# Decoder block, one core: first root with tokens on partitions, scale columns on ScalarE, fourth shift on VectorE, own tiles for early gate results, gated operands cast first

## The chip, the cores and the metric

The kernel runs on one core of a Trainium2 chip. The time is device time in microseconds (us) of one execution of the whole program. The engines are TensorE (PE: matmuls, and PEld: the loading of their stationary operands), VectorE (DVE), ScalarE (ACT), GpSimd (POOL), and SyncE (SP), which here issues most of the loads. Each engine works through its own instructions strictly in the order in which the program has them. An instruction that must wait for another engine or for a transfer holds up everything behind it on its own engine, also work whose operands are long there.

## The reference

One decoder layer on 1024 tokens of 1024 channels in float32: a token-mixing sub-layer and a SwiGLU sub-layer, each between two root-mean-square norms and modulated by a vector c (shift, scale and gate columns from `silu(c) @ ada_w + ada_b`).

```python
mod = silu(c) @ ada_w + ada_b
sh1, sc1, ga1, sh2, sc2, ga2 = split(mod, 6)
h = rmsnorm(x, pre_mix_g) * (1 + sc1) + sh1
proj = h @ w_in                         # conv, q/k/v and gate columns
u = depthwise_conv(u_val * sigmoid(u_gate))
y_conv = silu(layernorm(u)) @ w_conv_out
y_att = stick_breaking_attention(q, k, v) @ w_att_out
merged = sigmoid(g_conv) * y_conv + sigmoid(g_att) * y_att
x = x + ga1 * rmsnorm(merged @ w_o, post_mix_g)
h = rmsnorm(x, pre_ffn_g) * (1 + sc2) + sh2
gate, up = split(h @ w_ffn_in, 2)
x = x + ga2 * rmsnorm((silu(gate) * up) @ w_ffn_out, post_ffn_g)
```

## The kernel before

Activations lie transposed in SBUF, channels on the 128 partitions and tokens along the row, so the 1024 by 1024 activation is eight tiles `x0` to `x7`. Products in higher precision are split: an operand is cast on ACT to fp32r (the "hi" half, line 145 for most) and DVE takes the rest (the "lo" half, "operand minus hi"); a product then is three matmuls, hi by hi, hi by lo and lo by hi.

The program is written in an order and then placed by a static scheduler, which decides the order on each engine. Priorities (`tc.high_priority`, `pin`) and scheduling-only dependencies (`add_manual_dep` with `NoSync`, which fix an order and cost no wait on the chip) steer it. Tiles come from pools; a tag with `bufs=2` is a ring of two buffers, and a new tile of that tag waits until the oldest one's last reader is done. Pools are opened and closed one after the other, and what is closed gives its memory to the pools that follow.

Three places matter here.

**The start.** ACT squares x, PE sums the squares over the partitions by matmuls with a matrix of ones (`sums`, line 251, into `pvar`), so the sum of each token stands on all 128 partitions, in two halves of 512 tokens. ACT takes the root from each half, 128 by 512 elements (lines 334 and 335), DVE corrects it by a Newton step of three instructions on 128 by 512 elements for each half (lines 343 to 345) and multiplies x by scale column and root (`x_op`, line 300). ACT adds the shift column and casts (`hi_op`, line 303, tiles `hhi`), and DVE makes the lo half (`lo_op`, line 306, tiles `hlo`). The shift column of each of the eight tiles comes either from PE (`shift_pe`, line 284, with `shift_act` on ACT, line 288) or from a dot product on DVE (`dot_c`, line 121; `SH_DVE` says for which tiles: 5, 6 and 7). The scale columns always come from dot products on DVE, with a small instruction on line 295 behind each.

**The gates.** Gate products use a seven-product scheme for 2 by 2 blocks. `early(i, q)` makes the first of the products for the gate pair i ahead of the rest: a load of the weights (`ew`), a cast on ACT and its lo on DVE (tiles `a`, lines 145 and 414), 12 matmuls into a PSUM tile `k` (line 427), and an ACT instruction that takes the result out of PSUM into a tile `ee` (line 672) and stores it (line 673). There are 14 such results. The `ee` tiles come from the tag `sg`, two buffers that the sigmoid results (line 653) use too. Behind this, in a new pool `pg`, the kernel loads x back (16 loads `f<-xm_d` on SP), combines its parts on DVE (tiles `f`, lines 722 to 725), makes the operands `T1o` to `T4o` of them (cast on ACT, lo on DVE, line 708), and then does the other five products for each gate pair (`other_five`): weights `gw0a`, `gw0b` and so on are loaded, summed on DVE (tiles `gs`, lines 750 to 755), split into the operands `s1o` to `s4o` and `a` (line 414 for the lo), and multiplied with the T tiles on PE into `ka` and `kc`. The layer norm of the convolution branch (`ln_all`) is woven in: loads `cr<-u_d` on SP, sums on DVE (`la`, lines 795 and 797), a matmul `lnm` on PE (line 799), its copy `lm` on ACT (line 800), subtractions on DVE (`cr<-cr,lm`, line 803), squares, a matmul `lnv` (line 809), a root, and products (line 813).

**The FFN's down projection.** It opens with `prep1(j)` for j = 0 to 10: two gated operands `gb` from `X_j` (cast on ACT, lo on DVE, line 1577) and two weight operands `wa` (cast on ACT, lo on DVE, line 1583), then 24 matmuls on line 1591. `X` and `Y` are loaded back from `g_d`, the raw weights `wa` come from a ring of three buffers.

Of the kernel before, what the change touches and what calls it, by code (L numbers as in the profile page):

```python
# [69 lines left out]
def tile_block(ctx: ExitStack, tc: tile.TileContext, xT, vecs, ada1, ada2, win, wv, wcv, wat, wo, w1, w2, cvw, out):  # L70
# [126 lines left out]
    with ExitStack() as s0:  # L197
# [52 lines left out]
        def sums(src, c, first=False, last=False):  # L250
            pe.matmul(pvar[c], ones, src[:, hs[c]], start=first, stop=last)
# [27 lines left out]
        def shift_of(k):
            return mod[:, k:k + 1]  # L280

        def shift_pe(k):
            for kt in range(KT):
                pe.matmul(psh[:, k % 4], aws[k][:, 0, kt * P:(kt + 1) * P], csb[:, kt],
                          start=(kt == 0), stop=(kt == KT - 1))

        def shift_act(k):
            act.activation(shift_of(k), psh[:, k % 4, 0:1], AF.Identity, bias=vec[:, C_ADAB + k:C_ADAB + k + 1], scale=1.0)

        def dots(k):  # L290
            if k in SH_DVE:
                dot_c(aws[k][:, 0], cb, k)
# [2 lines left out]
            dve.scalar_tensor_tensor(scale1[:, k:k + 1], mod[:, KT + k:KT + k + 1], sc1[:, k:k + 1],
                                     vec[:, C_PRE1 + k:C_PRE1 + k + 1], op0=ALU.add, op1=ALU.mult)

        def x_op(k, cols=slice(0, T)):
            x = xs[k][:, cols]
            dve.scalar_tensor_tensor(x, x, scale1[:, k:k + 1], rstd[:, cols], op0=ALU.mult, op1=ALU.mult)  # L300
# [30 lines left out]
        shift_pe(0)  # L331
        for c in range(NCH):
            r, (m, a) = rstd[:, hs[c]], rt[c]
            act.activation(r, pvar[c], AF.Abs_reciprocal_sqrt, bias=eps, scale=1.0 / D)
            act.activation(m, pvar[c], AF.Identity, bias=eps, scale=1.0 / D)
        gg0b = {c: ps0.tile([P, CH], F32, tag="pvar", name=f"pgg0_{c}", bufs=2) for c in range(NCH)}
        dots(0)
        shift_act(0)
        w0_hi(0)
        shift_pe(1)  # L340
        for c in range(NCH):
            r, (m, a) = rstd[:, hs[c]], rt[c]
            dve.tensor_tensor(a, r, r, op=ALU.mult)
# [2 lines left out]
            x_op(0, hs[c])
            hi_op(0, hs[c])
            gemm_q(q0b, w0s[0], 0, HH, cs=(c,))
            if c == 0:
                shift_pe(2)  # L350
        dots(1)
# [1531 lines left out]
```

## Time and profile before

| | |
|---|---|
| times of three runs | 1392.28, 1389.63 and 1390.16 us, median 1390.16 us |
| profiled execution | 1390.05 us, of which the span from the first to the last instruction is 1388.3 us |
| clock granted to TensorE over the span | 0.997 |
| busy, of the span | PE 98%, PEld 83%, DVE 75%, ACT 47%, POOL 8% |
| moved by DMA | 265.01 MB, mean 191 GB/s |

A row of the timeline has the start, the duration, the engine, the line, the operation, what is written and what is read, how many such instructions follow one another in the row, and in square brackets how long the engine stood idle before it and what ended that. Rows of DMA on SP are issues: the transfer lands later. Matmuls overlap, so the spacing of their starts says how fast PE goes, not the duration of one.

### The profile page before, as it was taken

Reading aid. Unit: us, or ns where it says so; the run is one execution under the profiler, and the core shown is the slowest. Engines: PE = TensorE matmul, PEld = TensorE weight load, DVE = VectorE, ACT = ScalarE, POOL = GpSimd, SP = SyncE. Lnnn points to the kernel's source line nnn. Section 1 sums busy time; section 2 is a strip of 40 time slices with the busy share of each in tenths; the row PEclk is TensorE's granted clock in tenths of the full one; section 3 lists DMA queues with packets and bytes.
Section 4 is the critical chain, followed back from the end, with each engine's and each line's share of the span. In section 5 each row is a group of like instructions: output and inputs, shape, how many; then the busy total and the mean of one; then the engine's idle time right before and its main releaser. Section 6 shows DMA issues by size and latency. Waiting matters only on the chain.

```text
span 1388.3 us, 18714 instructions
## 1 busy us (share of the span) xinstructions
PE 1364.1 (98%) x6778; PEld 1147.2 (83%) x6778; DVE 1046.9 (75%) x1600; ACT 651.7 (47%) x1147; POOL 107.4 (8%) x247
## 2 busy tenths in 40 slices
PE   7999999999999999999999999999999999999996
PEld 4898888998987888888877888888888887888886
DVE  7998686775857888877597987778878766784355
ACT  6475565464546546313365543324445444334441
POOL 0100000000000011000012200001111110000002
PEclk9999999999999999999999999999999999999998
DMA  9512051141468646865746544457776779596736
GB/s 381 218 35 82 17 167 46 47 131 38 128 194 287 215 161 235 311 190 175 294 137 193 201 147 172 148 186 257 247 245 240 264 255 389 165 341 221 248 107 122
DMA packets 94940, 265.01 MB, mean 191 GB/s; under 512 B 10048, under 2 KB 21440, under 8 KB 93824
## 3 DMA queue, kind: packets, MB, share of 16 engines
q1 hardware_dynamic: 74352, 201.68, 43.3%
q0 software_dynamic: 17904, 57.42, 11.8%
q10 hardware_dynamic: 2592, 4.72, 0.9%
q8 instruction: 53, 0.87, 0.2%
q14 instruction: 39, 0.32, 0.1%
HBM read 192.74 MB, written 71.04 MB: 190 GB/s over the span
## 4 chain that ended last, share of the span: by engine, by line
PE 93%; DVE 2%; DMA 2%; ACT 1%; issue 1%; SPq 0%; DVEq 0%; ACTq 0%
PE ka L1044 15%; PE ka L1591 9%; PE kc L1044 8%; PE pwo L962 6%; PE ke L1153 4%; PE pb L1591 4%; PE ka L427 4%; PE pgv L166 3%; PE pyc L784 3%; PE pya L166 3%; PE kc L427 3%; PE pv L504 3%; PE pgg L166 2%; PE pk L166 2%; PE k L427 2%; PE pcv L483 2%
## 5 line engine op out<-in xcount | busy, mean ns | idle before, releaser
L578 ACT ACTIVATE ka<-z 128x128 f32<-128x128 f32 (+2 forms) x96 | 47.2, 494 | 44.3 <-PE z L577 35.1
L1591 PE MATMUL ka<-gt,w2f 128*128 128x512 f32 x264 | 63.4, 389 | 0.0
L584 DVE TENSOR_TENSOR_SCAN ka<-ka,eye 128x128 f32<-128x128 f32 (+1 forms) x64 | 51.4, 815 | 11.9 <-ACT ka L578 11.7
L589 DVE TENSOR_TENSOR be<-be,ka 128x127 f32<-128x127 f32 (+2 forms) x96 | 53.8, 572 | 7.1 <-ACT be L580 2.1
L1591 PEld LDWEIGHTS ka<-gt,w2f 128*128 128x128 f32 x264 | 49.5, 188 | 10.3
L121 DVE SCALAR_TENSOR_TENSOR ada<-ada,cb 128x1024 f32<-128x1024 f32 x32 | 39.1, 1223 | 22.1 <-DMA ada<-in_ada_dram 21.9
L580 ACT ACTIVATE be<-z 128x127 f32<-128x127 f32 (+2 forms) x96 | 46.9, 495 | 5.4 <-PE tr L602 5.2
L602 PE MATMUL tr<-ident,be 128*128 128x128 f32 x288 | 46.5, 272 | 0.5 <-DVE be L589 0.5
L1153 PE MATMUL ke<-b,w_hi 128*128 128x512 f32 x176 | 44.4, 394 | 0.0
L587 DVE TENSOR_TENSOR_SCAN ka<-ka 128x512 f32<-128x512 f32 x32 | 40.6, 1275 | 3.7 <-ACT ka L578 3.6
L483 PE MATMUL pcv<-ph,cvw 128*128 128x128 f32 x320 | 42.9, 275 | 0.0
L608 ACT ACTIVATE ahi<-tr 128x512 fp32r<-128x512 f32 x48 | 28.3, 600 | 27.5 <-PE tr L602 19.3
L483 PEld LDWEIGHTS pcv<-ph,cvw 128*128 128x128 f32 x320 | 40.4, 191 | 0.7
L1153 PEld LDWEIGHTS ke<-b,w_hi 128*128 128x128 f32 x176 | 33.0, 188 | 7.7 <-issue 1.0
L145 ACT ACTIVATE gt<-X 128x512 fp32r<-128x512 f32 x33 | 20.3, 629 | 39.2 <-DVE X L1634 14.2
L609 DVE TENSOR_TENSOR alo<-tr,ahi 128x512 fp32r<-128x512 f32 x48 | 32.1, 684 | 7.9 <-ACT ahi L608 7.6
L602 PEld LDWEIGHTS tr<-ident,be 128*128 128x128 f32 x288 | 34.8, 140 | 3.9 <-PE z L577 0.8
L145 ACT ACTIVATE s1o<-s 128x512 fp32r<-128x512 f32 x22 | 13.8, 629 | 51.3 <-PE ka L1044 43.7
L504 PE MATMUL pv<-wv_hi,hhi 128*128 128x256 f32 x128 | 36.8, 288 | 0.2 <-DVE klo L544 0.2
L504 PE MATMUL pv<-wv_hi,hlo 128*128 128x256 f32 x128 | 36.6, 286 | 0.0
L427 PE MATMUL k<-hhi,a 128*128 128x512 f32 x112 | 34.9, 390 | 1.4 <-ACT ee L672 1.4
L504 PE MATMUL pv<-wv_lo,hhi 128*128 128x256 f32 x128 | 36.2, 284 | 0.0
(551 smaller groups left out, 4155.5 us busy)
## 6 DMA issues: line engine op xcount, KB each, us to landing
w_d<-w2o POOLq DMA_DIRECT2D x44, 512.0 KB, 7.4
w2f<-w_d SPq DMA_DIRECT2D x44, 512.0 KB, 4.5
ada<-in_ada_dram SPq DMA_DIRECT2D x32, 512.0 KB, 5.1
w2r<-in_w_dram SPq DMA_DIRECT2D x44, 256.0 KB, 3.8
w1g<-in_w_dram SPq DMA_DIRECT2D x21, 512.0 KB, 3.7
w1u<-in_w_dram SPq DMA_DIRECT2D x21, 512.0 KB, 4.9
cvw<-in_cvw_dram SPq DMA_DIRECT2D x20, 512.0 KB, 3.7
ada_w<-in_ada_dram SPq DMA_DIRECT2D x8, 1024.0 KB, 13.7
```

What stands on the lines that cost most here:

```text
L166: pe.matmul(bank, st[:, cols], mv[k][:, c * CH:(c + 1) * CH], start=(i == 0 and s == 0), stop=(i == n - 1 and s == 2))
L427: pe.matmul(bank_, w[st][:, cols], mvs[mv], start=(first and j == 0 and s == 0), stop=(j == HK - 1 and s == 2), skip_group_check=not first)
L483: pe.matmul(cv[:, gi * TM:(gi + 1) * TM], wts[n][:, at:at + P], ph[:, g, SH - 1 - d:SH - 1 - d + TM], start=(d == 0), stop=(d == SH - 1))
L504: pe.matmul(pv[:, :256], st[k][:, tcols], mv[:, wc], start=(k == 0 and i == 0), stop=(k == KT - 1 and i == 2))
L578: act.activation(kap[:, s_lo:s_hi], z[:, zo:zo + w], AF.Sigmoid, bias=0.0, scale=-0.125)
L584: dve.tensor_tensor_scan(rev, rev, eye[:, CH - w:][:, ::-1], 0.0, op0=ALU.mult, op1=ALU.add)
L589: dve.tensor_tensor(beta[:, :m], beta[:, :m], kap[:, s_lo + 1:s_lo + 1 + m], op=ALU.mult)
L602: pe.transpose(tr[:, o:o + P], probs[ii][:, jo:jo + P], ident)
L962: pe.matmul(bank_, st[:, cols], mv[k][:, cs], start=(k == 0 and q == 0), stop=(k == KT - 1 and q == 2))
L1044: pe.matmul(bank_, st[:, cols], t[:, mv], start=(first and j == 0 and s == 0), stop=(j == HK - 1 and s == 2), skip_group_check=not first)
L1153: pe.matmul(kbs[f], wes[f][st][:, cols], t[:, mv], start=(i == 0 and j == 0 and st == 0 and mv == 0), stop=(j == HK - 1 and st == 1), skip ...
L1591: pe.matmul(dst, w[st][:, cols], g[mv], start=first and s == 0, stop=last and s == 2, skip_group_check=more)
```

## The change

Four edits, from the start of the kernel to its end.

1. The sums of the squares are formed with tokens on partitions: `sums` takes blocks of 128 by 128 of the squares as the stationary operand and the ones as the moving one, so the sums of 512 tokens stand as four columns. Root and Newton step then work on 128 by 4 elements (`roots`, `spread`). To bring the root back to all partitions, DVE multiplies the identity matrix by each of the four columns (`dr`) and PE multiplies ones by the result (`rb`); ACT copies `rb` into `rstd` (`keep`). The `x_op` of tile 0 reads `rb` in PSUM, the others `rstd`.
2. The scale columns (line 295 before) and the addition of the bias to the shifts that DVE makes are done on ACT (`scale_act`, `dots`). Shift 4 moves from PE to a dot product on DVE (`SH_DVE`).
3. The `ee` tiles come from pool `pa`, tags `ahi` and `alo`, two buffers each, and not from the tag `sg`.
4. In `prep1` for j = 0 to 2, the ACT instructions are chained by scheduling-only dependencies in the order of the source: `gb` ahead of `wa`, j by j.

```diff
-SH_DVE = (5, 6, 7)
+SH_DVE = (4, 5, 6, 7)
...
         def sums(src, c, first=False, last=False):
-            pe.matmul(pvar[c], ones, src[:, hs[c]], start=first, stop=last)
+            for b in range(4):
+                pe.matmul(pvar[c][:, b * P:(b + 1) * P], src[:, c * CH + b * P:c * CH + (b + 1) * P], ones,
+                          start=first and b == 0, stop=last and b == 3, skip_group_check=True)
...
-                dve.tensor_tensor(shift_of(k), shift_of(k), vec[:, C_ADAB + k:C_ADAB + k + 1], op=ALU.add)
+                act.activation(shift_of(k), shift_of(k), AF.Identity, bias=vec[:, C_ADAB + k:C_ADAB + k + 1], scale=1.0)
...
+        def scale_act(k):
+            act.activation(scale1[:, k:k + 1], mod[:, KT + k:KT + k + 1], AF.Identity, bias=sc1[:, k:k + 1],
+                           scale=vec[:, C_PRE1 + k:C_PRE1 + k + 1])
...
+            r = rstd[:, cols] if k else rb[0 if cols.start == 0 else 1]
+            dve.scalar_tensor_tensor(x, x, scale1[:, k:k + 1], r, op0=ALU.mult, op1=ALU.mult)
...
+        def roots(c):
+            s4 = pvar[c].rearrange("p (b n) -> p b n", n=P)[:, :, 0]
+            act.activation(r8[:, b4[c]], s4, AF.Abs_reciprocal_sqrt, bias=eps, scale=1.0 / D)
+            act.activation(m8[:, b4[c]], s4, AF.Identity, bias=eps, scale=1.0 / D)
+
+        def spread(c):
+            r, m, a = (t[:, b4[c]] for t in (r8, m8, a8))
             dve.tensor_tensor(a, r, r, op=ALU.mult)
             dve.scalar_tensor_tensor(a, m, -0.5, a, op0=ALU.mult, op1=ALU.mult)
             dve.scalar_tensor_tensor(r, a, 1.5, r, op0=ALU.add, op1=ALU.mult)
+            for b in range(4 * c, 4 * c + 4):
+                dve.tensor_scalar(dr[:, b * P:(b + 1) * P], ident, r8[:, b:b + 1], None, op0=ALU.mult)
+            pe.matmul(rb[c], ones, dr[:, hs[c]], start=True, stop=True)
+
+        def keep(c):
+            act.activation(rstd[:, hs[c]], rb[c], AF.Copy)
...
-                e = sgp.tile([P, CH], F32, tag="sg", name=f"ee{q}_{i}", bufs=2)
+                e = pa.tile([P, CH], F32, tag=("ahi", "alo")[q], name=f"ee{q}_{i}", bufs=2)
...
+        prep1_last = []
+
         def prep1(j, w):
+            n0 = len(nc.cur_bb.bb.instructions)
+            r = prep1_ops(j, w)
+            if j < 3:
+                last = prep1_last
+                for ins in nc.cur_bb.bb.instructions[n0:]:
+                    if ins.engine == mybir.EngineType.Activation:
+                        if last:
+                            tc.add_manual_dep(ins, last[-1], mybir.DependencyInfo(
+                                mybir.DependencyClass.NoSync, mybir.DependencyReason.SCHED_ONLY))
+                        last.append(ins.name)
+            return r
```

What the scheduler makes of it reaches further than the lines of the diff. Line numbers in the rows of the changed kernel are higher by 6 to 32.

**The loads that make the T operands.** Rows of SP, the queue of loads, behind the store `o_d` of the attention's last output. Before, the 16 loads `f<-xm_d` follow the fourth of the seven weight loads `ew` (rows with x2 are two loads):

```order
L98 DMA o_d_69<-oT_3553 128x1024
L98 DMA ew_4317<-in_win_dram 128x1024
L98 DMA f_0_4504<-xm_d_103 128x512 x2
L98 DMA f_0_4505<-xm_d_107 128x512 x2
L98 DMA f_1_4526<-xm_d_104 128x512
L98 DMA f_1_4527<-xm_d_104 128x512
```

In the changed kernel, at the same place:

```order
L98 DMA o_d_69<-oT_3593 128x1024
L98 DMA ew_4357<-in_win_dram 128x1024
L98 DMA ew_4396<-in_win_dram 128x1024
L98 DMA ew_4435<-in_win_dram 128x1024
L98 DMA ew_4474<-in_win_dram 128x1024
L98 DMA gw0a<-in_win_dram 128x1024
L98 DMA gw0b<-in_win_dram 128x1024
L98 DMA cr_4953<-u_d_74 128x1024
L98 DMA cr_4954<-u_d_75 128x1024
L98 DMA cr_4955<-u_d_76 128x1024
L98 DMA gw1a<-in_win_dram 128x1024
L98 DMA cr_4956<-u_d_77 128x1024
```

The row that follows the last of these is the first load of `f`: the 16 loads have moved behind ten others, four of which (`cr`) wait for matmuls of the last early gate pair on PE, whose operands held the memory that `cr` takes.

**What stands between the early products and the five others.** Rows of PE from the last early product `k` on. Before:

```order
L427 MATMUL k_4436<-hhi_290,a_6_4473 128x512
L427 MATMUL kc_4623<-T1o_4517,s1o_4637 128x512 x2
L427 MATMUL ka_4622<-T2o_4514,s2o_4617 128x512 x2
L427 MATMUL kc_4623<-T1o_4517,s1o_4637 128x512
L427 MATMUL kc_4623<-T1o_4541,s1o_4637 128x512 x3
```

In the changed kernel:

```order
L459 MATMUL k_4476<-hhi_321,a_6_4513 128x512
L831 MATMUL lnm_4966<-la,ones 128x512
L841 MATMUL lnv_4980<-la,ones 128x512
L459 MATMUL kc_4663<-T1o_4557,s1o_4677 128x512 x2
L459 MATMUL ka_4662<-T2o_4554,s2o_4657 128x512 x2
L459 MATMUL kc_4663<-T1o_4557,s1o_4677 128x512
L459 MATMUL kc_4663<-T1o_4581,s1o_4677 128x512 x3
```

The two layer-norm matmuls now stand ahead of the first product with a T operand. On DVE, the operand `s1o` that this product needs was made in the fourth row behind the last early operand `a_6`; rows of DVE before:

```order
L414 TENSOR_TENSOR a_6_4473<-ew_4434,a_6_4473 128x512
L750 TENSOR_TENSOR gs_0_4610<-gw0b 128x512
L751 TENSOR_TENSOR gs_0_4611<-gs_0_4610,gw0a 128x512
L753 TENSOR_TENSOR gs_0_4612<-gw0a,gw0b 128x512
L414 TENSOR_TENSOR s1o_4637<-gs_0_4610,s1o_4637 128x512
```

In the changed kernel the layer norm and the `f` rows follow `a_6`:

```order
L446 TENSOR_TENSOR a_6_4513<-ew_4474,a_6_4513 128x512
L827 TENSOR_TENSOR la<-cr_4953,cr_4954 128x512
L829 TENSOR_TENSOR la<-la,cr_4955 128x512
L829 TENSOR_TENSOR la<-la,cr_4956 128x512
L835 TENSOR_TENSOR cr_4953<-cr_4953,lm 128x512
L835 TENSOR_TENSOR cr_4954<-cr_4954,lm 128x512
L835 TENSOR_TENSOR cr_4955<-cr_4955,lm 128x512
L835 TENSOR_TENSOR cr_4956<-cr_4956,lm 128x512
L839 TENSOR_TENSOR la<-la,lm 128x512
L754 TENSOR_TENSOR f_0_4544<-f_0_4544 128x512
```

and the end of this stretch, further down on DVE, is

```order
L756 SCALAR_TENSOR_TENSOR f_3_4616<-f_3_4616,mod,f_3_4615 128x512
L782 TENSOR_TENSOR gs_0_4650<-gw0b 128x512
L740 TENSOR_TENSOR T4o_4611<-f_2_4593,T4o_4611 128x512
L827 TENSOR_TENSOR la<-cr_4953,cr_4954 128x512
L757 SCALAR_TENSOR_TENSOR f_3_4617<-f_3_4617,mod,f_3_4616 128x512
L783 TENSOR_TENSOR gs_0_4651<-gs_0_4650,gw0a 128x512
L785 TENSOR_TENSOR gs_0_4652<-gw0a,gw0b 128x512
L740 TENSOR_TENSOR T2o_4626<-f_3_4616,T2o_4626 128x512
L740 TENSOR_TENSOR T1o_4629<-f_3_4615,T1o_4629 128x512
L740 TENSOR_TENSOR T3o_4632<-f_3_4614,T3o_4632 128x512
L829 TENSOR_TENSOR la<-la,cr_4955 128x512
L446 TENSOR_TENSOR s1o_4677<-gs_0_4650,s1o_4677 128x512
```

From the first `cr<-cr,lm` (line 835) to this last row there are 51 instructions on DVE; before, the same `f` and T work stood ahead of `a_6`. ACT has the same order: the cast of `s1o` stands behind the casts of T1, T2 and T3 of the last `f`.

**The start of the down projection.** Rows of ACT around the first gated operand `gb_0`. Before:

```order
L145 ACTIVATE wa_0_10319<-wa_10301 128x512
L1450 ACTIVATE uw_10129<-kc_10127 128x512
L145 ACTIVATE wa_1_10355<-wa_10304 128x512
L145 ACTIVATE wa_1_10358<-wa_10304 128x512
L145 ACTIVATE wa_2_10394<-wa_10307 128x512
L1468 ACTIVATE uw_10129<-uw_10129 128x512
L145 ACTIVATE wa_2_10397<-wa_10307 128x512
L145 ACTIVATE gb_0_10310<-X_10270 128x512
L145 ACTIVATE gb_0_10313<-X_10270 128x512
```

In the changed kernel:

```order
L1482 ACTIVATE uw_10169<-kc_10167 128x512
L1500 ACTIVATE uw_10169<-uw_10169 128x512
L145 ACTIVATE gb_0_10350<-X_10310 128x512
L145 ACTIVATE gb_0_10353<-X_10310 128x512
L145 ACTIVATE wa_0_10356<-wa_10341 128x512
L145 ACTIVATE wa_0_10359<-wa_10341 128x512
L145 ACTIVATE gb_1_10389<-X_10311 128x512
```

The gated operands come first, and the casts of the weights have moved from the stretch before the uw row to behind it. A fourth raw weight tile needs the buffer of `wa_0`, so its load can be issued only when the casts and lo halves of `wa_0` are done. On SP, where this load `wa_10346` stood ahead of the load of `Y_2` (`Y_10283`), it (`wa_10386`) now stands behind all loads of `X` and `Y`:

```order
L98 DMA Y_10330<-g_d_120 128x2x512
L98 DMA X_10319<-g_d_120 128x2x512
L98 DMA Y_10331<-g_d_121 128x2x512
L98 DMA X_10320<-g_d_121 128x2x512
L98 DMA wa_10386<-in_w_dram 128x1024
L98 DMA wa_10425<-in_w_dram 128x1024
```

It has moved behind eleven loads that it stood ahead of.

More of the change, by code (lines that the diff above doesn't have):

```diff
@@ L211, in tile_block @@
         pvar = [ps0.tile([P, CH], F32, tag="pvar", name=f"pvar{c}", bufs=2) for c in range(NCH)]
-        psh = ps0.tile([P, 4, P], F32, name="psh")
+        psh = {}
         csb = p0.tile([P, KT, P], F32, name="csb")
@@ L216, in tile_block @@
         sc1 = small.tile([P, KT], F32, name="sc1")
+        r8, m8, a8 = (small.tile([P, KT], F32, name=f"{nm}8") for nm in "rma")
         warm = small.tile([P, 1], F32, name="warm")
@@ L235, in tile_block @@
         dve.tensor_tensor(csil, csil, vec[:, C_CCOL:C_CCOL + KT], op=ALU.mult)
-        dve.tensor_scalar(sc1, vec[:, C_ADAB + KT:C_ADAB + 2 * KT], 1.0, None, op0=ALU.add)
+        dve.scalar_tensor_tensor(sc1, vec[:, C_ADAB + KT:C_ADAB + 2 * KT], 1.0, vec[:, C_PRE1:C_PRE1 + KT],
+                                 op0=ALU.add, op1=ALU.mult)
         act.activation(warm, eps, AF.Abs_reciprocal_sqrt, bias=eps, scale=0.0)
@@ L330, in tile_block @@
         pe_begin = len(nc.cur_bb.bb.instructions)
[L331 to L342, printed above, removed]
+        b4 = [slice(4 * c, 4 * c + 4) for c in range(NCH)]
+        def roots(c):
[4 more added lines that the diff above has]
+            r, m, a = (t[:, b4[c]] for t in (r8, m8, a8))
             dve.tensor_tensor(a, r, r, op=ALU.mult)
@@ L345, in tile_block @@
             dve.scalar_tensor_tensor(r, a, 1.5, r, op0=ALU.add, op1=ALU.mult)
[L346 to L351, printed above, removed]
+            for b in range(4 * c, 4 * c + 4):
[3 more added lines that the diff above has]
+            act.activation(rstd[:, hs[c]], rb[c], AF.Copy)
+        roots(0)
+        dots(0)
+        roots(1)
+        gg0b = {c: ps0.tile([P, CH], F32, tag="pvar", name=f"pgg0_{c}", bufs=2) for c in range(NCH)}
+        w0_hi(0)
+        shift_pe(0, 0, 4)
+        spread(0)
+        keep(0)
+        shift_pe(0, 4)
+        shift_act(0)
+        spread(1)
+        x_op(0, hs[0])
+        hi_op(0, hs[0])
+        gemm_q(q0b, w0s[0], 0, HH, cs=(0,))
+        shift_pe(1)
+        keep(1)
+        dots(1, False)
+        x_op(0, hs[1])
+        hi_op(0, hs[1])
+        gemm_q(q0b, w0s[0], 0, HH, cs=(1,))
+        shift_pe(2)
+        scale_act(1)
         w0_lo(0)
@@ L1650, in load1, with prep1_ops @@
             return w
+        prep1_last = []
         def prep1(j, w):
+            n0 = len(nc.cur_bb.bb.instructions)
[9 more added lines that the diff above has]
+            return r
+        def prep1_ops(j, w):
             x = X[j]
```

20 lines of the change are left out of this document (11 added, 9 removed).

## The prediction

> **What bounds the kernel now.** I read the busy shares first, then the chain of work that ended last, then what PE waits for.
>
> ```profile
> PE 1364.1 (98%) x6778; PEld 1147.2 (83%) x6778; DVE 1046.9 (75%) x1600; ACT 651.7 (47%) x1147; POOL 107.4 (8%) x247
> PE 93%; DVE 2%; DMA 2%; ACT 1%; issue 1%; SPq 0%; DVEq 0%; ACTq 0%
> PE k L427 <- ACT ee L672: 1.4, 1, 1.4
> PE ka L1591 <- ACT gb L145: 1.2, 1, 1.2
> ```
>
> PE is busy for 98% of the span and carries 93% of the chain. So the rule for every edit is: what it saves on DVE or ACT is worth only the PE wait that it shortens, and a new PE wait costs its whole length, because no later PE idling exists in which it could be won back. Edits 3 and 4 aim at the two waits shown, of 1.4 and 1.2 us. The decisive place is where edit 3 has moved other work, behind the early products:
>
> ```profile
> 458.35 0.39 PE L427 MATMUL k<-hhi,a 128*128 128x512 f32 x1
> 458.57 0.62 PE L427 MATMUL kc<-T1o,s1o 128*128 128x512 f32 x2
> 458.00:470.00 12.00, 12.00 (x53) 9.58 (x52) 9.93 (x18) 5.70 (x10) 0.00 (x0) 1.00 0.69 274
> ```
>
> The first product with a T operand starts 0.22 us after the last early product, at 458.57, which I call E, and PE is busy for all 12 us of the window (its first column after the length). This holds because all T work was done long before, under the early products:
>
> ```profile
> 409.45 9.15 SPq L98 DMA_DIRECT2D f<-xm_d  x14
> 419.22 0.69 DVE L708 TENSOR_TENSOR T2o<-f,T2o 128x512 fp32r<-128x512 f32 x1
> 435.36 0.75 DVE L725 SCALAR_TENSOR_TENSOR f<-f,mod,f 128x512 f32<-128x512 f32 x1
> 454.94 0.63 ACT L145 ACTIVATE s1o<-gs 128x512 fp32r<-128x512 f32 x1 [1.01 <-DVE gs L750]
> ```
>
> The loads were issued from 409.45 on, 49 us ahead of E, and `s1o` was cast at 454.94. From 419.22 to 435.36 DVE starts 27 instructions of this kind, one every 0.62 us (16.14 over 26).
>
> **The change part by part. Edits 1 and 2 (start).** Here DVE, working without a pause, feeds PE until the last `x_op` and its `hhi`:
>
> ```profile
> 18.66 0.22 DVE L295 SCALAR_TENSOR_TENSOR scale<-mod,sc,vec 128x1 f32<-128x1 f32 x1
> 18.79 0.69 DVE L343 TENSOR_TENSOR nr<-rstd 128x512 f32<-128x512 f32 x1
> 21.04 0.75 DVE L300 SCALAR_TENSOR_TENSOR x<-x,scale,rstd 128x512 f32<-128x512 f32 x1
> 10.78 1.65 DVE L266 TENSOR_SCALAR csb<-ones,csil 128x128 f32<-128x128 f32 x8
> 43.33 1.22 DVE L121 SCALAR_TENSOR_TENSOR ada_w<-ada_w,cb 128x1024 f32<-128x1024 f32 x1
> 57.49 1.15 ACT L303 ACTIVATE hhi<-x,mod 128x1024 fp32r<-128x1024 f32 x1 [3.97 <-DVE x L300]
> 32.28 2.05 PE L284 MATMUL psh<-csb,ada_w 128*128 128x128 f32 x16 [0.35 <-ACT mod L288]
> ```
>
> From DVE go two Newton chains of 2.25 us (18.79 to 21.04), eight scale rows at 0.13 us (18.66 to 18.79) and three bias additions of some 0.1: 5.8 us. To it come eight products with the identity, by the row of eight like ones 1.65 us, six instructions on 128 by 4 elements, at 0.2 each 1.2 us, and one dot of 1.3 us with its read-out: 4.15 us. Net 1.65 us less. Against it stand two new waits: the `x_op` halves of tile 0 wait for the spread matmul and ACT's copy, some 1.5 us each, mostly beside other DVE work; I leave 0.45 us of them uncovered. PE loses the 2.05 us of shift 4, but at the last `hhi` DVE decides, so PE's gain is DVE's: **-1.2 us**. Bounds: -2.1 (all of PE's row) and -0.3 (both waits half uncovered). The sums in blocks of 128 cost PE the same columns; their price I take as nothing within these bounds.
>
> **Edit 3, the wait that goes.** With four buffers `ee` waits neither for its stores nor behind the T casts, which have left that stretch of ACT: **-1.4 us**, the wait shown.
>
> **Edit 3, the wait that comes.** In the changed order the 16 `f` loads stand on SP behind the `cr` loads, which wait for PE. When those go is in the trace:
>
> ```profile
> 451.06 1.33 SPq L98 DMA_DIRECT2D cr<-u_d  x3
> 453.21 0.82 SPq L98 DMA_DIRECT2D cr<-u_d  x1
> 463.09 0.69 DVE L797 TENSOR_TENSOR la<-la,cr 128x512 f32<-128x512 f32 x1 [2.04 <-DMA cr<-u_d]
> 464.02 1.02 PE L799 MATMUL lnm<-la,ones 128*128 128x512 f32 x2
> 465.74 0.58 ACT L800 ACTIVATE lm<-lnm 128x512 f32<-128x512 f32 x1
> f<-xm_d SPq DMA_DIRECT2D x16, 256.0 KB, 5.4
> cr<-u_d SPq DMA_DIRECT2D x4, 512.0 KB, 6.9
> gw0a<-in_win_dram SPq DMA_DIRECT2D x1, 512.0 KB, 3.5
> gw1b<-in_win_dram SPq DMA_DIRECT2D x1, 512.0 KB, 5.6
> ```
>
> So no `f` load leaves before about 454, against 409.45. On PE nothing stands between the last early product and the first T product but `lnm` and `lnv`, and on DVE 51 instructions stand from the first `cr<-cr,lm` to the lo half of `s1o`, which PE's second step needs. All times below are on the clock of before, so E is 458.57:
> - the last `cr` lands at 463.09 as now (its issue does not move); `la` is done at 463.78, `lnm` takes 1.02, `lm` 0.58: the 51 instructions start at 465.5;
> - 50 steps of 0.62 and the last one's 0.69 are 31.7 us: 497.2;
> - within them one load is waited for. The last two `f` loads go when the T2 and T1 lo halves of the second `f` are done (so they do now: the pair below). Between that T2 lo and the reader stand six steps, 3.7 us, and the load lands after 5.4: 1.8 us with its issue. `s1o` lo is done at **499.0**, 40.4 us after E;
> - PE then has 24 matmuls; the next operand is `s2o` of the second gate pair, whose weights `gw1b` are loaded into the buffer of `gw0b`, by the program's counts only when the lo half of `a_0` is done, four steps on: 501.5. Issue and landing 5.9, two sums 1.4, cast 0.63, lo 0.69: **510.1**. From here PE has 72 matmuls in hand and does not run dry.
>
> ```profile
> 424.88 0.69 DVE L708 TENSOR_TENSOR T2o<-f,T2o 128x512 fp32r<-128x512 f32 x1
> 425.60 1.53 SPq L98 DMA_DIRECT2D f<-xm_d  x2
> ```
>
> Between E and 510.1, 51.5 us, PE does 26 matmuls at 0.227 (12 in 2.72 us, from the rows 1171.21 and 1173.93 below) and three layer-norm matmuls at 0.63 (464.02 to the next product at 464.65): 7.8 us. Idle: 43.7 us.
>
> To this comes what a restart costs. The trace has no long gap in mid-kernel, but PE's very first group has one before it:
>
> ```profile
> 4.16 3.75 PE L244 MATMUL cbp<-dia,ones 128*128 128x512 f32 x4 [4.16 <-DVE dia L241]
> 13.52 1.98 PE L251 MATMUL pvar<-sq,ones 128*128 128x512 f32 x4 [0.56 <-ACT sq L248]
> ```
>
> Four records of one shape take 3.75 us after 4.16 us of idling and 1.98 later: 1.77 us more. Two restarts bear on the end, `lnm` (about half of its 1.8, as it is short) and the one at 510; the one at 499 is hidden by the wait for `gw1b`. Together 2.7 us, with 0 as the other bound; I take 2.7, as the only row with a gap has it.
> [...]
>
> So **+46.4 us**. Bounds: low 36 (no restart cost, -2.7; no wait for `f`, -1.8; `gw1b` in 3.5, -2.1; the last `cr` landing 6.9 after its issue as the median, -2.9; steps of 0.60, -1), high 54 (`f` and `gw1b` each as late as the last `cr`, which took 9.9 us: +4.5 and +4.3, with -1 of overlap).
>
> **Edit 4 (down projection).**
>
> ```profile
> 1157.00 0.63 ACT L1468 ACTIVATE uw<-uw 128x512 f32<-128x512 f32 x1
> 1159.00 0.69 DVE L1484 TENSOR_TENSOR p<-ka,p 128x512 f32<-128x512 f32 x1 [0.64 <-PE ka L1044]
> 1160.20 1.19 PE L1591 MATMUL ka<-gb,wa 128*128 128x512 f32 x4 [1.24 <-ACT gb L145]
> 1170.33 0.52 SPq L98 DMA_DIRECT2D X<-g_d  x1
> DMA to landing us min/median/max: 3.6/10.3/12.1
> 1171.21 2.88 PE L1591 MATMUL ka<-gb,wa 128*128 128x512 f32 x12
> 1173.93 2.88 PE L1591 MATMUL pa<-gb,wa 128*128 128x512 f32 x12
> 1170.00:1175.00 5.00, 5.00 (x24) 4.14 (x23) 1.21 (x3) 0.00 (x0) 0.00 (x0) 1.00 1.05 397
> ```
>
> The `gb` casts can now follow the uw row at 1157.63, and the first matmul can start at about 1159.4. But the second needs `gb`'s lo half, and DVE makes it behind the `p` row, 1159.69, which waits for PE itself: 1160.35. The wait of 1.2 us changes its cause, and **-0.2 us** is left. Against it, the fourth weight tile `wa_3` is now loaded behind the last `X`, so from 1170.9 on. The row of landings is that of `wa`: median 10.3 us. PE comes to this tile after three times 24 matmuls, 1160.2 + 16.4 = 1176.6. By the median it lands at 1181.2 and costs, with its cast of 0.6, 5.2 us; but three loads of the same burst now stand behind it and not ahead, 1.5 MB, some 3.9 us at the 397 GB/s of the window (its last column). I take +2.6, bounds 0 and 5.5. Together **+2.4 us**, bounds -0.5 and 5.5.
>
> Sum: -1.2 - 1.4 + 46.4 + 2.4 = +46.2 on the profiled execution's 1390.05 us, which is within 0.1 us of the median: **1436 us**.
>
> **The rivals.**
> - *The cover holds (the other side).* If `s1o`'s lo half were done by E, the wait would not come: 1390.05 - 1.2 - 1.4 = 1387.4, or 1390 with the `wa_3` wait. It decides at 40 us: the `f` loads would have to go out by about 413. For it speaks that they did before, at 409.45; against it, that SP takes its rows in order and `cr` is issued at 451.
> - *Part of the wait is given back*, because PE's second product finds its operands ahead of the lo halves, or DVE steps are shorter than 0.6: between 1395 and 1421. Against it: PE has no idle time behind E in which to catch up (the window's 12.00 of 12.00).
> - *No restart cost*: 1433.5; it lies inside the range.
> - *The gate loop stays short of weights behind 510*: each further pair's loads go out only when DVE has done the pair before, 14 steps of 0.62 and a landing of 5.6, 14.3 us against 13.6 of PE work (60 matmuls). 0.7 us for five pairs is 3.5: 1440, also inside. Above 1448 only if a landing of 10 us recurs at each.
> - *The own tiles do nothing for the 1.4 us*: 1437.5.
>
> **How the numbers follow.** The range takes the low bounds together, 1390.05 - 2.1 - 1.5 + 36 - 0.5 = 1422, and the high ones, 1390.05 - 0.3 - 1.2 + 54 + 5.5 = 1448. I give 0.80 to the forecast with the cases inside the range (0.2 of it to no restart cost), 0.04 to the cover holding, 0.08 to a part given back, 0.08 to longer than 1448. A measurement of this kernel can tell about 0.2%, 2.8 us, from no change. The cover case is split between faster (0.03) and same (0.01); all others are slower.
>
> **What would show it.** Right: PE idle for over 30 us in one piece behind the last `k` product, released by ACT `s1o` or DVE `s1o`, the `f` rows of DVE behind `la`, `f` loads behind `cr` on SP; a second wait of some us for `s2o` with `gw1b` behind it; no wait at `k<-hhi,a`; a wait for `wa` at the fourth tile of the down projection; the last `hhi` of the start about 1 us earlier. Wrong: T products that start within a few us of the last `k`, or DVE steps far from 0.62 us.

## The result, and the profile after

The changed kernel takes 1433.99 us (median of 6 runs, 1429.06 to 1435.76), the kernel before 1389.95 us on the same chip: a ratio of 1.031, interval 1.0293 to 1.0327. The profiled execution of the changed kernel has a span of 1432.2 us, 43.9 us more than before. From its page, the row of granted clock by slices and the shares of the chain of work that ended last:

```profile
PEclk9999999999998599999999999999999999999998
...
PE 86%; DVE 7%; DMA 3%; ACT 2%; issue 1%; SPq 0%; DVEq 0%; ACTq 0%
```

DVE has 7% of the chain where it had 2%, and one slice (465.4 to 501.2 us) has a granted clock of 0.54. Which place that is, PE's waits say (total, times, longest, in us):

```profile
PE kc L459 <- ACT s1o L145: 19.4, 1, 19.4
PE lnv L841 <- DVE la L839: 6.3, 1, 6.3
PE lnm L831 <- DVE la L829: 6.0, 1, 6.0
...
PE ka L1623 <- ACT gb L145: 2.9, 1, 2.9
```

The first three are one gap with the two layer-norm matmuls in it. The timeline of PE there, from the last early product on:

```profile
454.07 0.39 PE L459 MATMUL k<-hhi,a 128*128 128x512 f32 x1
460.48 2.04 PE L831 MATMUL lnm<-la,ones 128*128 128x512 f32 x2 [6.02 <-DVE la L829]
468.81 2.08 PE L841 MATMUL lnv<-la,ones 128*128 128x512 f32 x2 [6.29 <-DVE la L839]
490.30 1.22 PE L459 MATMUL kc<-T1o,s1o 128*128 128x512 f32 x2 [19.41 <-ACT s1o L145]
...
494.77 4.31 PE L459 MATMUL kc<-T1o,s1o 128*128 128x512 f32 x10 [1.73 <-DVE s1o L446]
498.91 2.48 PE L459 MATMUL ka<-T2o,s2o 128*128 128x512 f32 x10
...
502.96 3.29 PE L459 MATMUL ka<-T2o,s2o 128*128 128x512 f32 x12 [0.71 <-ACT s2o L145]
```

Before, the first T product started 0.22 us behind the last early one. Let E' be 454.30, the same 0.23 us behind the start of the last `k`. PE is then all but idle for 40 us. The windows (length, then busy time of PE, PEld, DVE, ACT, POOL, then the granted clock as the third number from the end) show DVE busy for 40.92 of 50 us while PE has 15.54:

```profile
454.00:504.00 50.00, 15.54 (x36) 7.99 (x35) 40.92 (x66) 19.84 (x33) 0.00 (x0) 0.59 0.51 177
```

Where the 43.9 us came from is read by the first start of the same product in both traces: `pv` behind the start, `k` the early products, `pya` behind the gate loop, `pb` behind the opening of the down projection. These are the groups of the changed kernel (duration, then first and last start); before, the first starts were 64.6, 418.8, 601.0 and 1282.7:

```profile
L536 PE MATMUL pv<-wv_hi,hhi x128: 274/283/368, 61.9 to 283.7; 128*128 128x256 f32 x128
...
L459 PE MATMUL k<-hhi,a x112: 388/389/389, 416.2 to 454.1; 128*128 128x512 f32 x112
...
L166 PE MATMUL pya<-ohi,wa_hi x64: 389/389/389, 639.8 to 682.2; 128*128 128x512 f32 x64
...
L1623 PE MATMUL pb<-gb,w2f x132: 389/389/389, 1326.6 to 1383.5; 128*128 128x512 f32 x132
```

The start gives 2.6 us, the early products 1.7 (their last `k` moved from 458.35 to 454.07), the gate loop takes 43.1, and the stretch to `pb` 5.1: together +43.9.

### The profile page after: what moved, and what is told of

The parts are those of the page before. It is cut to its first block, busy times and chain, and to the rows that moved or that the text cites. A ratio compares the mean times of both kernels' runs of the same rounds, so it can differ in the third digit from the quotient of the medians.

```text
span 1432.2 us, 18810 instructions
## 1 busy us (share of the span) xinstructions
PE 1372.7 (96%) x6826; PEld 1153.6 (81%) x6826; DVE 1044.3 (73%) x1599; ACT 655.0 (46%) x1160; POOL 107.1 (7%) x247
## 4 chain that ended last, share of the span: by engine, by line
PE 86%; DVE 7%; DMA 3%; ACT 2%; issue 1%; SPq 0%; DVEq 0%; ACTq 0%
PE ka L1076 15%; PE kc L1076 8%; PE ka L1623 8%; PE pwo L994 6%; PE ke L1185 4%; PE pb L1623 4%; PE pgv L166 3%; PE pya L166 3%; PE pyc L816 3%; PE ka L459 3%; PE pv L536 3%; PE pgg L166 2%; PE pk L166 2%; PE k L459 2%; PE pcv L515 2%; PE pq L166 2%
## 5 line engine op out<-in xcount | busy, mean ns | idle before, releaser
L616 DVE TENSOR_TENSOR_SCAN ka<-ka,eye 128x128 f32<-128x128 f32 (+1 forms) x64 | 51.5, 816 | 12.0 <-ACT ka L610 11.6
L1623 PEld LDWEIGHTS ka<-gt,w2f 128*128 128x128 f32 x264 | 49.6, 188 | 10.3
L634 PE MATMUL tr<-ident,be 128*128 128x128 f32 x288 | 46.4, 272 | 0.5 <-DVE be L621 0.5
L459 PE MATMUL kc<-T1o,s1o 128*128 128x512 f32 x84 | 23.8, 423 | 21.1 <-ACT s1o L145 19.4
L515 PEld LDWEIGHTS pcv<-ph,cvw 128*128 128x128 f32 x320 | 40.4, 191 | 0.7
L459 PEld LDWEIGHTS kc<-T1o,s1o 128*128 128x128 f32 x84 | 17.0, 207 | 27.1 <-ACT s1o L145 21.2
L1623 PE MATMUL ka<-gb,wa 128*128 128x512 f32 x132 | 34.1, 405 | 4.1 <-ACT gb L145 2.9
```

The costliest lines, as they stand in the source:

```text
L459: pe.matmul(bank_, w[st][:, cols], mvs[mv], start=(first and j == 0 and s == 0), stop=(j == HK - 1 and s == 2), skip_group_check=not first)
L515: pe.matmul(cv[:, gi * TM:(gi + 1) * TM], wts[n][:, at:at + P], ph[:, g, SH - 1 - d:SH - 1 - d + TM], start=(d == 0), stop=(d == SH - 1))
L616: dve.tensor_tensor_scan(rev, rev, eye[:, CH - w:][:, ::-1], 0.0, op0=ALU.mult, op1=ALU.add)
L634: pe.transpose(tr[:, o:o + P], probs[ii][:, jo:jo + P], ident)
L1623: pe.matmul(dst, w[st][:, cols], g[mv], start=first and s == 0, stop=last and s == 2, skip_group_check=more)
```

## The experiments

Line numbers in rows of variants without edits 1 and 2 are those of before. Times are medians.

**e2, edits 1 and 2 alone** (in the changed kernel, `ee` from the tag `sg` again and no chain in `prep1`).

```diff
-                e = pa.tile([P, CH], F32, tag=("ahi", "alo")[q], name=f"ee{q}_{i}", bufs=2)
+                e = sgp.tile([P, CH], F32, tag="sg", name=f"ee{q}_{i}", bufs=2)
...
-        prep1_last = []
```

> Edits 1 and 2 alone. Theory: -2.6 us, the lead that PE had at the first pv matmul of the changed kernel (61.95 against 64.57), carried to the end, since PE bounds the rest: 1387.4 us. Rival (the lead is lost at the 1.4 us wait for ee and later, because other engines set the pace there): 1389 to 1390 us.

1388.21 us, ratio 0.998 (0.9971 to 0.999). The interval, some 1386.4 to 1389.1 us, holds the 1387.4 of the theory and also the 1389 of the rival, so how much of the lead of 2.6 us is lost on the way is not decided. The two small waits that edits 3 and 4 aim at are still there, the first longer than before:

```profile
PE k L459 <- ACT ee L704: 2.1, 1, 2.1
PE ka L1623 <- ACT gb L145: 1.2, 1, 1.2
```

**e3, edit 4 alone, and e4, edit 3 alone** (before, with the one edit each).

> Edit 4 alone. Theory (the late load of the fourth weight tile costs more than the earlier gated operands bring): PE waits some 3 us ahead of the fourth pair of the down projection, 1390 + 5 = 1395 us at most, 1393 at least. Rival (the wait of 2.9 us in the changed kernel comes from the later phase of the transfers there, not from the order): no wait at the fourth tile, 1389 to 1390 us.

> Edit 3 alone. Theory: -1.6 us (no wait for ee) and +43 us (PE idle behind the early products until the s1o lo half, some 40 us after the last k product): 1431.5 us. Rival (the idling needs the earlier start or the other order of the down projection): under 1420 us.

e3 takes 1395.99 us, ratio 1.0035 (1.0022 to 1.0048), 1 us above the most that was expected, and waits 2.9 us at the fourth weight tile. e4 takes 1430.87, ratio 1.0282 (1.0266 to 1.0297). Against the 1390.48 us of before on the same chip the three parts are -2.3, +5.5 and +40.4, sum 43.6; the changed kernel stood 44.0 above the kernel before on its own chip. The edits do not interact by more than these runs can tell.

**e1, all but edit 3** (the first line pair of e2's diff alone).

> The changed kernel with edit 3 alone undone: the ee tiles come from the tag sg again, edits 1, 2 and 4 stay. Theory (the ee tiles in pool pa push the f loads behind cr, and PE's long idling follows from that alone): f loads back behind the fourth ew, no idling above 2 us behind the last k product, time 1390 - 2.6 (start, as measured on PE in the changed kernel) + 5 (down projection, as measured there) = 1392.5 us. Rival (the start's edits shift the schedule and edit 3 only adds to it): 1415 us or more, with PE waiting behind the last k product.

1393.27 us, ratio 1.002 (1.001 to 1.0029): edit 3 is where the loss is. Its `f` loads leave from 407.90 on, near the 409.45 of before.

**e5 and e6: one, and seven, of the 14 early results from pool `pa`**, the rest from `sg` (edits 1 and 2 in, edit 4 out).

```diff
+                e = (pa if len(ees) < 1 else sgp).tile([P, CH], F32, tag=("ahi", "alo")[q] if len(ees) < 1 else "sg", name=f"ee{q}_{i}", bufs=2)
```

> Edits 1 and 2, without edit 4, and of the 14 ee tiles only the first taken from pool pa; the other 13 come from the tag sg as before. Theory (what counts is how long pool pa is held by an ee tile, since the f tiles lie in the pool that takes its memory): the first f loads stay behind the fourth ew, PE has no wait behind the last k product, and the first ee no longer stands behind the T casts on ACT, so the wait of 1.4 us goes as well: start only - 1.5 = 1386.7 us. Rival (any ee tile in pa brings the idling): 1425 us or more.

> As the one before, with the first seven of the 14 ee tiles from pool pa. The first f loads stand behind the last ew. Theory (the price grows with the time that pa is held): the loads leave some 30 us later than before but 15 us earlier than in the changed kernel; 32 DVE steps of 0.62 us then end some 8 to 10 us behind the last k product, PE waits in pieces of some us at T products: 1392 to 1398 us. Rival (all or nothing): 1387 or 1428.

Both missed. e5 takes 1393.83 us, ratio 1.0027 (1.0018 to 1.0036): the first `ee`'s wait is gone, but others come in its place. Even one tile from `pa` changes the order: the `f` loads are now spread between the weight loads `ew`. Its SP queue:

```profile
407.11 6.84 SPq L98 DMA_DIRECT2D f<-xm_d  x4
423.93 0.33 SPq L98 DMA_DIRECT2D ew<-in_win_dram  x1
424.36 7.54 SPq L98 DMA_DIRECT2D f<-xm_d  x8
```

and PE's waits in e5:

```profile
PE k L459 <- ACT a L145: 2.9, 2, 2.0
PE kc L459 <- ACT s1o L145: 1.7, 1, 1.7
```

The longest of the first two stands behind an `ee` on ACT that waits 2.14 us (to 441.86) for the store of an earlier result. Whether the spread loads or the order of the rows on ACT and DVE make these waits was not separated.

e6 takes 1415.28, ratio 1.0181 (1.0165 to 1.0197), well past its expectation: the loads stand behind all `ew` (434.82), and the wait for `s1o` is 9.1 us with others behind it. With none, one, seven and all 14 in `pa` and edit 4 out, the times are 1388.2, 1393.8, 1415.3 and, as an estimate, 1428 (the changed kernel less e3's +5.5). So it is not all or nothing; what each single tile costs was not run.

**e7, the gap filled.** 26 matmuls, whose result nobody reads, are written behind the last early product of the changed kernel, to see whether PE's slow stretch comes from idling. On PE 16 of them stand behind it, ten ahead of its end.

```diff
+            wb = bank("k_warm")
+            for n in range(26):
+                pe.matmul(wb, hhi[HK + n % HK][:, :P], hhi[HK + n % HK][:, :CH], start=True, stop=True)
```

> The changed kernel with 26 matmuls of 128x512 fp32r more behind the early products, whose results nobody reads, so that PE has some 4 us of work in the first 6 us gap. If idling slows PE afterwards, lnm takes 1.02 us there as it does in the kernel before (2.04 in the changed kernel), lnv, with its gap of 6 us unfilled, still 2.08. If lnm is slow for another reason (its operand, a port), it stays at 2.04. The time changes by 1 us at most in either case.

One run, 1434.26 us. The rows of `lnm` and `lnv`, to be compared with those above:

```profile
460.09 1.02 PE L834 MATMUL lnm<-la,ones 128*128 128x512 f32 x2
469.33 2.08 PE L844 MATMUL lnv<-la,ones 128*128 128x512 f32 x2 [8.22 <-DVE la L842]
```

Without the idle time ahead of it `lnm` takes 1.02 us and not 2.04; behind the gaps that remain, `lnv` (2.08 us, 1.02 in before) and the first ten `kc` products (4.09 us, where ten take 2.43 in before) stay slow. So in these two kernels the idle time ahead of it is what slows `lnm`. The kernel gains nothing that one run can show: `lnv` now waits 8.22 us, where it waited 6.29.

**e8 and e9: a smaller form of edit 4.** Only the casts of `wa_1` are placed behind `gb_0`; e8 on e5, e9 on e2.

```diff
+            acts = [ins for ins in nc.cur_bb.bb.instructions[n0:] if ins.engine == mybir.EngineType.Activation]
+            if j == 0:
+                gb0_last.append(acts[1].name)
+            elif j == 1:
+                for ins in acts[2:]:
+                    tc.add_manual_dep(ins, gb0_last[0], mybir.DependencyInfo(
+                        mybir.DependencyClass.NoSync, mybir.DependencyReason.SCHED_ONLY))
```

> As e5, with another order at the down projection: only the casts of wa for j = 1 are made to follow those of gb_0, so wa_0 is cast early and its buffer comes free, and the fourth weight tile is loaded ahead of the Y tiles as before. Theory (in edit 4 the late load of the fourth weight tile is the loss, the order of gb against wa_1 and wa_2 the small gain): no wait at the fourth tile, 0 to 1 us below e5: 1386.2 us. Rival (the gated operands first lose by themselves): 1388 us or more.

> Edits 1 and 2, the ee tiles from the tag sg as before, and the order of e8 at the down projection. If the three parts are independent, it keeps e2's gain and has no wait of 1.2 us at the first gated operand: e2's 1388.2 - 1.1 = 1387.1 us, 0.9975 of before. If the order of e8 brings nothing, 1388.2.

e8: 1393.62 us, ratio 1.0022 (1.0013 to 1.0031), 0.2 below e5, where 0 to 1 was expected; the 1386.2 us named for it were missed because e5 had missed its own. e9: 1388.3, ratio 0.9983 (0.9974 to 0.9992), no difference from e2 that can be measured and not the 1387.1 us of its theory. The late load is gone, but the wait of 1.2 us for `gb`'s cast has become one of 0.9 us for its lo half.

**e10: e9, with the T casts placed behind the first two `ee` on ACT**, by the same kind of dependency.

```diff
+            if j >= 1:
+                for ins in nc.cur_bb.bb.instructions[n0:]:
+                    if ins.engine == mybir.EngineType.Activation:
+                        for k_ in (0, 1):
+                            tc.add_manual_dep(ins, ees[k_], mybir.DependencyInfo(
+                                mybir.DependencyClass.NoSync, mybir.DependencyReason.SCHED_ONLY))
```

> e9 and scheduling-only dependencies that put the T casts of the second to fourth f behind the first two ee on ACT. If the wait of some 2 us ahead of the third early product comes from those four casts standing ahead of the first ee (and not from the two buffers of the tag sg), it goes: e9 - 2 = 1385 us. If it comes from the buffers, it stays, with the store of sg as what is waited for: 1387.

1387.58 us, ratio 0.9976 (0.9966 to 0.9986), by its median the lowest of all versions, though the interval overlaps those of e2 and e9. Two waits are left of what edits 3 and 4 aimed at:

```profile
PE ka L1630 <- DVE gb L1616: 0.9, 1, 0.9
PE k L459 <- ACT ee L704: 0.9, 1, 0.9
```

The order on ACT took 0.5 us or more of the wait for `ee`: it was 1.4 in e9 and 2.1 in e2, two kernels that are the same up to there, so a single trace sizes it only roughly. What is left is the rival cause, the two buffers of the tag `sg`: the first `ee` no longer stands behind T casts on ACT, but waits for a store out of that tag:

```profile
422.94 0.60 ACT L704 ACTIVATE ee<-k 128x512 f32<-128x512 f32 x1 [3.56 <-DMA s_d<-sg]
```

So both causes are real, and the time missed the 1385 us of the first.

**e11: the `f` loads on another queue.** All else as in the changed kernel.

```diff
-                load(b, xm_d[k][:, c * CH:(c + 1) * CH])
+                nc.gpsimd.dma_start(b, xm_d[k][:, c * CH:(c + 1) * CH])
```

> The changed kernel, with the 16 loads of f issued by GpSimd on its own queue and not by SP; nothing stands ahead of them on that queue. Only the row in which they leave is asked for. Theory (the early results hold pool pa's memory, which the f tiles take, so the loads wait for the last early pair whatever the queue): the first f loads leave later than 440 us, and the whole takes 1420 to 1437 us. Rival (they are late only because SP has ten other loads ahead of them): the first f loads leave between 400 and 415 us. The time alone does not decide it: in this order DVE still has the layer norm's sums ahead of the f rows, so even by the rival s1o's lo half ends only a few us sooner, 1428 to 1434 us.

The theory falls. One run took 1438.55 us, above the ranges of the theory and of the rival, and these are the issues on GpSimd's queue:

```profile
388.29 2.71 POOL L752 DMA_DIRECT2D f<-xm_d  x5 [0.40 <-issue]
394.02 1.07 POOL L752 DMA_DIRECT2D f<-xm_d  x2 [3.02 <-DVE be L621]
409.95 3.71 POOL L752 DMA_DIRECT2D f<-xm_d  x7 [14.86 <-DMA o_d<-oT]
```

14 of the 16 loads leave by 414, ahead of the first early result, so in this kernel the memory of these `f` tiles was free. And it helps nothing, because on DVE the first `f` row still stands behind the layer norm:

```profile
462.52 2.49 DVE L835 TENSOR_TENSOR cr<-cr,lm 128x512 f32<-128x512 f32 x4 [2.75 <-ACT lm L832]
...
466.33 0.68 DVE L754 TENSOR_TENSOR f<-f 128x512 f32<-128x512 f32 x1
...
494.86 0.68 DVE L446 TENSOR_TENSOR s1o<-gs,s1o 128x512 fp32r<-128x512 f32 x1
```

The first row marked `f` here starts some 53 us after the last of the 14 loads left (466.33 against 413.66), and `s1o`'s lo half ends at 495.54, 40.8 us after E' (454.75 here). The 4.6 us above the changed kernel are in part another order of rows further on: PE waits 2.7 us for a `gv` row of DVE, which it did not there.

**e12: e11, with the layer norm's first row on DVE placed behind the last T lo half** (`t_lo` lists the T lo halves).

```diff
+                first = dve.tensor_tensor(s0_, cr[0][:, cs], cr[1][:, cs], op=ALU.add)
+                if c == 0:
+                    tc.add_manual_dep(first.ins, t_lo[-1], mybir.DependencyInfo(
+                        mybir.DependencyClass.NoSync, mybir.DependencyReason.SCHED_ONLY))
```

> The kernel of e11 (f loads on GpSimd's queue), with the first row of the layer norm on DVE put behind the last lo half of the T operands by one scheduling-only dependency. The scheduler then leaves the layer norm behind the operands s1o to a_0 of the first gate pair on DVE and its matmuls behind the first gate products on PE, but the casts of T still stand on ACT behind the read-out of the last early product. Theory (the loads are not what is late; the wait is the length of the chain that stands between the last early product and s1o on DVE): the chain is now 27 rows from the first T lo half to s1o's lo half, not 51 behind the layer norm's matmul: it starts some 1.3 us after the end of the last early product, and 26 steps of 0.62 us later s1o's lo half is done, 18 us after that end where it was 40.4; no second wait for gw1b, since PE then has 60 matmuls in hand, 13.6 us; so the time falls by some 24 us to 1410 us (1404 to 1416). Rival (the wait has a part that hangs on the pool's memory or on the cr loads, and not on the rows between): s1o's lo half is not done before 30 us after that end, and the time stays above 1420 us.

1416.88 us, ratio 1.0183 (1.0166 to 1.02): 17 us come back against the changed kernel; 24 were expected, 1404 to 1416 us. The mechanism holds. Rows of DVE:

```profile
451.89 0.75 DVE L758 SCALAR_TENSOR_TENSOR f<-f,mod 128x512 f32<-128x512 f32 x1
457.65 0.69 DVE L740 TENSOR_TENSOR T2o<-f,T2o 128x512 fp32r<-128x512 f32 x1 [5.01 <-ACT T2o L145]
...
474.29 0.68 DVE L446 TENSOR_TENSOR s1o<-gs,s1o 128x512 fp32r<-128x512 f32 x1
```

The first `f` is made by 452.6 and then waits 5.01 us for ACT, where the T cast stands behind the read-out of the last early product (455.99). From there the chain ends at 474.97, 19.2 us after E' (455.80 here), where 18 was expected. What was missed is PE's speed afterwards:

```profile
472.62 1.22 PE L459 MATMUL kc<-T1o,s1o 128*128 128x512 f32 x2 [16.67 <-ACT s1o L145]
475.03 3.78 PE L459 MATMUL kc<-T1o,s1o 128*128 128x512 f32 x8 [1.19 <-DVE s1o L446]
...
480.31 2.76 PE L459 MATMUL ka<-T2o,s2o 128*128 128x512 f32 x10
```

From 475.03 to 480.31 PE starts 12 matmuls in 5.28 us (granted clock 0.50 over 475.0 to 478.6 us), where 12 take 2.72 at a granted clock of 1.00: 2.6 us, with no second wait to hide them. Three waits of about a microsecond further on in the gate loop (0.9 to 1.0 each) and a last `k` that starts 1.5 us later than in the changed kernel are of the size of the rest.

## Why the prediction was right

The forecast of 1436 us lies 2 us above the median. Part of that closeness is luck: its four terms were off by -1.4, -0.3, -3.3 and +2.7 us, which cancel down to -2.3. The steps, one by one:

- **The start, -1.2: mis-sized, the runs show -2.6** (first `pv`; e2: -2.3). The last `hhi` starts 2.33 us sooner than the 57.49 of before:

```profile
55.16 1.16 ACT L315 ACTIVATE hhi<-x,mod 128x1024 fp32r<-128x1024 f32 x1 [2.08 <-DVE x L312]
```

  The prediction priced the rows that leave DVE at their starts' distance, 0.13 us for a scale row. Between successive tiles DVE's first dot now comes after 4.69 us (40.91 to 45.60) and not 5.13: 0.44 a tile. The rows show where it comes from, before and after:

```profile
44.73 1.28 DVE L306 SCALAR_TENSOR_TENSOR hlo<-x,mod,hhi 128x1024 fp32r<-128x1024 f32 x1
...
43.20 1.29 DVE L318 SCALAR_TENSOR_TENSOR hlo<-x,mod,hhi 128x1024 fp32r<-128x1024 f32 x1
```

  Before, a dot's sum is read out at 44.47, the scale row follows at 44.59 and `hlo` at 44.73, 0.26 us behind the read-out; a bias row costs 0.20 in the same way (43.13 to 43.33). After, the read-out is at 43.20 and `hlo` starts with it. So the rows that left took the gaps ahead of them along (0.26 and 0.20 us here, of the 0.44 a tile that came out). An estimate: eight scale rows at 0.26 and three bias rows at 0.20, not 0.13 and 0.10, are 1.3 us more, the size of the miss.
- **Edit 3, the wait that goes, -1.4: right** (-1.7).
- **Edit 3, the wait that comes, +46.4: right in its mechanism, 3.3 too much** (+43.1). `s1o`'s lo half was predicted 40.4 us after E; its row, 494.00 below, ends at 494.71, 40.4 us after E'. That agreement is two errors that cancel: the layer norm's part came later (the chain's first row at 463.19, 8.9 us after E', predicted 6.9), and the wait of 1.8 us for the last `f` did not come, since the load, issued at 478.18, was there at 481.72. About 1 us of the layer norm's delay is `lnm` at a granted clock of 0.50 (2.04 us, not 1.02). Rows of DVE:

```profile
463.19 2.50 DVE L835 TENSOR_TENSOR cr<-cr,lm 128x512 f32<-128x512 f32 x4 [2.86 <-ACT lm L832]
...
481.72 0.76 DVE L755 SCALAR_TENSOR_TENSOR f<-f,dsh,f 128x512 f32<-128x512 f32 x1
...
494.00 0.71 DVE L446 TENSOR_TENSOR s1o<-gs,s1o 128x512 fp32r<-128x512 f32 x1
...
500.82 0.69 DVE L782 TENSOR_TENSOR gs<-gw1b 128x512 f32<-128x512 f32 x1 [1.11 <-DMA gw1b<-in_win_dram]
...
502.94 0.69 DVE L446 TENSOR_TENSOR s2o<-gs,s2o 128x512 fp32r<-128x512 f32 x1
```

  The second term, the wait for `gw1b`, was mis-sized: it was issued at 497.1 and read at 500.82, 3.7 us, not 5.6, so `s2o`'s lo half ended 49.3 us after E' and not 51.5, 2.2 less. Of the restart cost of 2.7 us nothing came on top: the part at `lnm` is real, but lies in the layer norm's delay above, and the one behind the wait for `gw1b` did not come, since PE had got its speed back under the 20 matmuls between (granted clock 1.00 over 499 to 503 us). Against these two stands a wait of 1.69 us later in the gate loop, which the sum did not have: -3.2 of the -3.3. The row that the restart cost was taken from, PE's first group in before, is slow at a granted clock of 1.00 (4.16 to 7.70 us), and `lnm` at one of 0.50: that the two have one cause is not shown.
- **A wrong reason inside it.** The sum starts at the landing of `cr` and counts the rows of DVE, and that held. But the prediction let the wait begin with the `f` loads behind `cr` on SP, and its rival was to be decided by them: "the `f` loads would have to go out by about 413". In e11, 14 of the 16 had gone out by 413.7, and the cover did not hold: the order of DVE's and ACT's rows gives the same 40 us with the loads early. e12 moves, from there, only the layer norm on DVE and halves them. With the loads late and the layer norm moved no kernel was run. In all three kernels the first T cast stands behind the last early result. Why the scheduler places it there stays open: that it holds the rows of pool `pg` back until `pa` is released would fit e5 and e6, but in e12 the `f` rows on DVE, tiles of `pg` too, stand ahead of that result's read-out (449.59 against 455.99). SP itself stood 3.9 us ahead of its first `f` load in the changed kernel, by the profile for the store of an early result; whether that wait belongs to these loads was not shown. The 19 us that are left in e12 were not taken apart further.
- **Edit 4, +2.4: right in its mechanism, half the size** (+5.1; e3: +5.5). The late load is the cause that was named, and the wait that it makes, 2.90 us, is near the 2.6 that were priced. The term that failed is the slow stretch behind the wait: the prediction counted a restart behind the early products and none here. The load and its cast on ACT:

```profile
1206.66 17.08 SPq L98 DMA_DIRECT2D wa<-in_w_dram  x5
...
1217.22 0.63 ACT L145 ACTIVATE wa<-wa 128x512 fp32r<-128x512 f32 x1 [11.77 <-DMA wa<-in_w_dram]
```

  The landing took 10.5 us, about the median of 10.3 that the prediction had quoted; there was no gain from a shorter queue. But the load went out 8.9 us before PE ran out of work (at 1215.5), where the prediction had 5.7 (1170.9 to 1176.6). The two cancel, so the 2.6, which the prediction had not worked out from its 5.2 and 3.9, came out right by luck. PE then pays twice:

```profile
1218.42 0.51 PE L1623 MATMUL ka<-gb,wa 128*128 128x512 f32 x1 [2.90 <-ACT gb L145]
1219.23 4.16 PE L1623 MATMUL ka<-gb,wa 128*128 128x512 f32 x11 [0.30 <-DVE gb L1609]
1223.23 2.89 PE L1623 MATMUL pa<-gb,wa 128*128 128x512 f32 x12
```

  the wait of 2.90 us, and 12 matmuls that take 4.81 us (1218.42 to 1223.23, with a short wait of 0.30 in it) where 2.72 is their time at a granted clock of 1.00: 5.0 in all.
- **The rivals.** "The cover holds" was refused by the trace. "Part of the wait is given back" did not come: PE stood for 40 us. "No restart cost" names 1433.5 us, 0.5 from the measured time, and is refused all the same by `lnm` (2.04 us, and 1.02 in e7): the number fits because other terms were off. "The gate loop stays short of weights" did not come. There is one wait of 1.69 us at 560.96 for the lo half of an `s2o`, but its weights had been read from 555.30 on without a wait; on DVE the lo half, at 560.22, stands behind a row of the layer norm:

```profile
558.30 2.08 DVE L862 TENSOR_TENSOR lm<-cr,la 128x1024 f32<-128x1024 f32 x1
```

  "The own tiles do nothing" is wrong: the `ee` wait did go.

## What to carry to other kernels

Giving a tile a new home also changes how long that pool lives, and a static scheduler may move what comes after the pool; look at the order of every engine's rows behind the last reader before counting the wait that goes. A wait of 1 to 2 us can have two causes, as here the order on ACT and the buffers: a new order of a few rows is the smaller change and can be tried first. A price for a wait of PE may need a slow stretch behind it as well: here a wait of 2.90 us cost 5.0, and one of 1.69 us left the granted clock at 1.00. When a transfer looks late, ask what its first reader stands behind: moving the transfer alone gave nothing here; with one row of the reader's engine moved as well it gave 17 us.

## What the runs showed of the hardware

Behind a wait of 2.90 us PE ran at a granted clock of 0.50. Windows of the changed kernel around the wait at the fourth weight tile (the granted clock is the third number from the end):

```profile
1215.50:1218.40 2.90, 0.02 (x1) 0.00 (x0) 0.52 (x1) 1.18 (x3) 0.00 (x0) 1.00 0.51 202
1218.40:1222.40 4.00, 3.69 (x9) 2.74 (x10) 4.00 (x8) 4.00 (x8) 0.00 (x0) 0.57 0.38 102
1222.50:1226.00 3.50, 3.50 (x17) 2.86 (x16) 3.46 (x7) 1.70 (x4) 0.00 (x0) 1.00 0.47 165
```

In this wait the clock is still 1.00 through the idle time. Finer windows give 0.97 from 1218.40 to 1218.80, 0.50 from there to 1222.00, 0.76 to 1222.40, and then 1.00 again: some 3.2 us at 0.50. In the longer gap ahead of `lnm` it fell within the gap: 1.00 over 456 to 457 us, 0.80 over the next one and 0.50 over 458 to 459. In e3 the same wait, 2.87 us, is followed by 12 matmuls in 5.67 us (1181.13 to 1186.80); the wait of 1.69 us at 560.96 in the changed kernel left the granted clock at 1.00. What a wait of a length between these does is left open here. So 1.8 of the 5.0 us that the late load cost are not waiting, and they stand in no row of waits.

Two loads of 512 KB landed after 3.7 us (`gw1b`; from its issue to its landing the DMA share was 0.67, at 189 GB/s) and after 10.5 us (`wa`; ten loads of `X` and `Y` had been issued in the 16 us ahead of it, and the share was 1.00, at 379 GB/s). What the trace of before gave for the same tiles, 5.6 and 10.3 us, held for the second and not for the first.
